# Weight tiles of a hybrid SSD/GLA decoder step: a ring of six half tiles, each with its own transfer, in place of three whole ones

## The chip, the cores and the metric

The kernel runs on one core of one Trainium2 chip. The metric is the device time of one execution in microseconds (us). A core has TensorE (PE, matmuls; its weight loads are the profile's row PEld), VectorE (DVE), ScalarE (ACT) and GpSimd (POOL), and SyncE (SP), which here only issues transfers. Transfers issued by SP and by POOL run on the same 16 DMA engines. PE reads its operands from the on-chip memory (SBUF) and writes accumulators (PSUM).

## The reference

One decoder layer over a prompt of 256 tokens and eight sample sequences of 4 tokens, 288 columns in all, with the same weights: parallel Mamba-2 (SSD) and GLA branches, gated and merged, cross-attention into 256 memory tokens, and a convolutional FFN. Cut to what matters here, the products with weights:

```python
p_mem_k, p_mem_v = _mem_kv(mem_prompt, norm_mem, w_ck, w_cv)
...
xn = _rmsnorm(x, p['norm_mix'])
z, xbc, dt_raw, q, k, v, r, g_lr, gate_a, gate_b = _split(xn @ p['w_in'], IN_SIZES)
...
branch_a = u @ p['w_ssd_out']
...
branch_b = o @ p['w_gla_out']
merged = jax.nn.sigmoid(gate_a) * branch_a + jax.nn.sigmoid(gate_b) * branch_b
h = x + merged @ p['w_mix_out']
h = h + _cross_attend(_rmsnorm(h, p['norm_cross']), mem_k, mem_v, p['w_cq'], p['w_co'])
up = _rmsnorm(h, p['norm_ffn']) @ p['w_up']
up, ffn_conv_new = _causal_dwconv(up, ffn_conv, p['ffn_conv_w'], p['ffn_conv_b'])
a, gt = jnp.split(up, 2, axis=-1)
h = h + (jax.nn.silu(gt) * a) @ p['w_down']
```

Everything is float32. The model width is 2048, the FFN's 5632 (11264 columns of `w_up`).

## The kernel before

Every weight is read from HBM once, as float32, and split into two float32r parts, `whi` (the rounded weight) and `wlo` (what is left); activations are kept split the same way. A product is three matmuls: `whi` with the high part (L147), `whi` with the low part (L148), `wlo` with the high part (L151).

`wload` (L108) gives one raw tile: a buffer of the pool tag `raw`, of which there are RB = 3, and a transfer on SP's queue (L114). `proj_w` (L132) walks over k, the rows of the weight, in tiles of four blocks of 128 rows by 256 columns, 512 KB. It splits each tile in two steps of two blocks: `wsplit` (L100) has ACT cast `whi` (L103) and DVE subtract `wlo` (L105), both 128x512, from five buffers each (WB = 5). For each step PE runs 2 column tiles x 2 blocks x 3 = 12 matmuls of 128 x 288. Two steps share one raw tile, so its buffer is free for the next load when the second step's `wlo` has been computed.

`mem_proj` (L299) computes the memory's keys and values. Its tiles are two blocks of 128 rows by 512 columns, 512 KB too, split block by block; the very first tile is loaded with one transfer for each block (`apart`), since nothing else can start before it. `dt_load` (L482) fills a raw tile of 112 columns for the time steps and the GLA gate with two small transfers (L485) and repeats some columns on POOL (L488).

The order of work on each engine is set by the program's scheduler, which runs a timeline simulation of the instructions; the first `mem_proj` is kept in the order written. Generators of projections are woven with the scans (`weave`, L178), so that PE has matmuls between dependent steps. SP's queue is in order: a load that waits for a buffer holds all that is queued behind it, the state's stores (L915, L1199) among them, and a store that waits for its data holds the loads behind it. POOL's queue carries the loads of states, caches and memory.

Names that the prediction uses: `sin` are rows of the SSD state, updated on DVE (L910) and stored by SP (L915). `xqm` are masked copies of the sample queries in cross-attention (L1508), which ACT and DVE make and the score matmuls (L1529) read; `os` (L1610), `co` and `qh` (L194) are copies and splits in the same place. `sz` (L652) is the activated gate of an SSD group.

Of the kernel before, what the change touches and what calls it, by code (L numbers as in the profile page):

```python
# [16 lines left out]
P = 128  # L17
# [13 lines left out]
FT = FF // P  # L31
BLK = 8
NSQ = 2
RB = 3
WB = 5
STOP = object()
LNEXP = "natural_log_exp_and_others"
# [5 lines left out]
def hybrid_step(ctx: ExitStack, tc: tile.TileContext, I: dict, O: list):  # L43
    ctx.enter_context(tc.block(schedule_with_timeline_sim=True))
    nc = tc.nc
# [15 lines left out]
    def acc_tiles(n):  # L61

        turn[0] += 1
        return [ps.tile([P, 512], F32, tag=f"acc{turn[0] % 2}", bufs=2, name="acc") for _ in range(n)]
# [35 lines left out]
    def wsplit(raw):  # L100

        hi = wp.tile(list(raw.shape), F32R, tag="whi", bufs=WB, name="whi")
        S.copy(hi, raw)  # L103
        lo = wp.tile(list(raw.shape), F32R, tag="wlo", bufs=WB, name="wlo")
        V.tensor_tensor(lo, raw, hi, ALU.subtract)  # L105
        return hi, lo

    def wload(src, apart=False):  # L108
        raw = wp.tile([P, src.shape[1], src.shape[2]], F32, tag="raw", bufs=RB, name="raw")
        if apart:  # L110
            for k in range(src.shape[1]):
                nc.sync.dma_start(out=raw[:, k, :], in_=src[:, k, :])
        else:
            nc.sync.dma_start(out=raw, in_=src)  # L114
        return raw

    late = []
# [9 lines left out]
    def flush():  # L127

        while late:
            late.pop(0)()  # L130

    def proj_w(load, ncol, X, nk, cons, N=T):  # L132

        nt = (ncol + P - 1) // P
        accs = acc_tiles(nt)
        for k0 in range(0, nk, 4):
            kn = min(4, nk - k0)
            raw = load(k0, kn)
            for s0 in range(0, kn, 2):
                hi, lo = wsplit(raw[:, s0:s0 + 2, :])  # L140
                for j in range(nt):
                    m = min(P, ncol - j * P)
                    a = accs[j][0:m, 0:N]
                    cs = slice(j * P, j * P + m)
                    for k in range(2):
                        xh, xl = X(k0 + s0 + k)
                        MM(a, hi[:, k, cs], xh, start=(k0 + s0 + k == 0), stop=False)  # L147
                        MM(a, hi[:, k, cs], xl, start=False, stop=False)  # L148
                    for k in range(2):
                        xh, xl = X(k0 + s0 + k)  # L150
                        MM(a, lo[:, k, cs], xh, start=False, stop=(k0 + s0 + k == nk - 1))  # L151
                    if k0 + s0 + 2 == nk:
                        cons(j, a)
                if k0 + s0 == min(4, nk - 2):
                    flush()
                yield
# [7 lines left out]
    def proj(w, c0, ncol, X, nk, cons, row0=0):  # L164
        def load(k0, kn):
            return wload(rows_of(w, row0, k0, kn, c0, ncol))
        return proj_w(load, ncol, X, nk, cons)
# [104 lines left out]
    with pool("p0") as p0:  # L272
# [9 lines left out]
        def mem_load(k0):  # L282
            cs = slice(k0 * P, (k0 + 2) * P)
            nc.sync.dma_start(out=mt[:, :, cs], in_=I["mem_prompt"][0, :, cs].rearrange("(i p) c -> p i c", p=P))
# [14 lines left out]
        def mem_proj(w, hd, dst, prep=None, hold=None):  # L299

            def feed():
                for k0 in range(0, KT, 2):
                    if prep is not None:
                        mem_load(k0)
                    raw = wload(w[k0 * P:(k0 + 2) * P, 512 * hd:512 * hd + 512].rearrange("(k p) n -> p k n", p=P),
                                prep is not None and k0 == 0)
                    for k in range(2):
                        if prep is not None:
                            prep(k0 + k)
                        yield wsplit(raw[:, k:k + 1, :])  # L310

            accs = acc_tiles(2)
            ws = feed()
            ready = [next(ws) for _ in range(2)] if prep is not None else []
            for kk in range(KT):
                if prep is None:
                    ready.append(next(ws))
                hi, lo = ready.pop(0)
                for m in range(2):
                    ms_ = slice(m * P, (m + 1) * P)  # L320
                    MM(accs[m], mn_hi[:, kk, ms_], hi[:, 0, :], start=(kk == 0), stop=False)  # L321
                    MM(accs[m], mn_lo[:, kk, ms_], hi[:, 0, :], start=False, stop=False)  # L322
                for m in range(2):
                    ms_ = slice(m * P, (m + 1) * P)
                    MM(accs[m], mn_hi[:, kk, ms_], lo[:, 0, :], start=False, stop=(kk == KT - 1))  # L325
                if prep is not None:
                    ready += [w_ for w_ in (next(ws, None) for _ in range(2 if kk == 0 else 1)) if w_]
                yield

            def rows():  # L330
                t = p0.tile([P, 2, 512], F32, tag="mp", bufs=2, name="mp")
                for m in range(2):
                    S.activation(t[:, m, :], accs[m], ACT.Identity, scale=mrs[:, m:m + 1])
                G.dma_start(out=dst[0, :, hd, :].rearrange("(m p) d -> p m d", p=P), in_=t)
            if hold is None:
                rows()
            else:
                hold.append(rows)
# [143 lines left out]
        def dt_load(k0, kn):  # L482
            raw = wp.tile([P, kn, 112], F32, tag="raw", bufs=RB, name="raw")
            for o, c0, n in ((0, O_DT, 32), (32, O_G, 16)):
                nc.sync.dma_start(out=raw[:, :, o:o + n],  # L485
                                  in_=rows_of(I["w_in"], 0, k0, kn, c0, n))
            for k in range(kn):
                G.tensor_copy(raw[:, k, 48:112].rearrange("p (r n) -> p r n", n=16),  # L488
                              raw[:, k, 32:48].unsqueeze(1).to_broadcast([P, 4, 16]))
            return raw  # L490

        def dt_cons(j, a):
# [4 lines left out]
            V.tensor_tensor(lr3[64:80, :], a[64:80], lr3[64:80, :], ALU.subtract)  # L497

        run(proj_w(dt_load, 112, X, KT, dt_cons))

        def dt_prep():
# [908 lines left out]
    for j2 in range(KT // 2):  # L1410
        def cons(j, a, j2=j2):
            added(hx[j2][:, j, :], 2 * j2 + j, a, vec("norm_cross"), hn, acc)
# [238 lines left out]
    for i in range(5):  # L1651
        src = I["ffn_conv_w"][i] if i < 3 else I["ffn_conv_b"] if i == 3 else I["norm_final"]
# [246 lines left out]
```

## Time and profile before

| | us |
|---|---|
| three runs: median (lowest to highest) | 2500.24 (2498.2 to 2500.59) |
| the profiled execution | 2500.31 |
| its span (from the first to the last recorded instruction) | 2498.6 |

How to read it: the span is what the profile's shares refer to; some 1.7 us of the profiled execution lie around it. Busy time of PE is the union of its matmuls, whose ends are modelled. "Idle before" in a row is the time that the engine stood still just ahead of that instruction, and the arrow names what it waited for.

| Stage | from, to (us) | what runs |
|---|---|---|
| memory keys and values | 0 to 186 | `w_ck`, `w_cv`; the input's norm; dt and gate columns at 113 to 122 |
| SSD branch | 186 to 700 | columns of `w_in`, four groups' scans, `w_ssd_out` |
| GLA branch and gates | 700 to 1280 | columns of `w_in`, four heads' scans, `w_gla_out` |
| mix | 1280 to 1380 | `w_mix_out` |
| cross-attention | 1380 to 1646 | `w_cq`, scores and values, `w_co` |
| FFN | 1646 to 2476 | `w_up`, `w_down`, in blocks of eight |
| final norm and stores | 2476 to 2499 | |

The granted clock of PE was 0.997 over the whole span. SP's queue moved 422.35 MB in 408512 packets, POOL's 102.93 MB in 36512.

### The profile page before, as it was taken

The page shows a single profiled execution, that of the slowest core. Times are in us where ns is not written, and L with a number is a line of the kernel's source. Part 1 is how long each engine was busy: PE and PEld are TensorE (multiplying, and loading weights), DVE is VectorE, ACT ScalarE, POOL GpSimd, SP SyncE. Part 2 cuts the span into 40 slices and gives each one's busy share as a digit, 9 for nine tenths or more (in the row PEclk, how much of TensorE's full clock was granted, in tenths as well). Part 3 has the DMA queues.
Part 4 walks back from the last instruction along what each step waited for, and adds up shares of the span by engine and source line. Part 5 has one row for each costly group of instructions (what it writes and reads, how often), then busy time and mean ns, then how long its engine had stood idle before and what let it go on. Part 6 is the DMA issues. An engine that isn't in the chain of part 4 may idle for free.

```text
span 2498.6 us, 50407 instructions
## 1 busy us (share of the span) xinstructions
PE 2480.6 (99%) x18794; PEld 2398.5 (96%) x18794; DVE 1769.2 (71%) x3788; ACT 1332.1 (53%) x2717; POOL 445.3 (18%) x792
## 2 busy tenths in 40 slices
PE   9999999999999999999999999999999999999998
PEld 8889999999999999999999989999999999999998
DVE  6756777797877666777666577667777677675766
ACT  6656647656464655544444545555555454454545
POOL 3102133342311010110111122402111011020012
PEclk9999999999999999999999999999999999999999
DMA  8776587777869686877778599655555555555556
GB/s 246 250 226 203 165 250 203 238 203 221 256 207 290 191 266 188 250 227 237 214 228 271 186 329 334 196 163 173 171 170 171 171 170 172 169 172 170 169 172 171
DMA packets 445302, 528.51 MB, mean 212 GB/s; under 512 B 28492, under 2 KB 391852, under 8 KB 445024
## 3 DMA queue, kind: packets, MB, share of 16 engines
q1 hardware_dynamic: 408512, 422.35, 55.3%
q0 software_dynamic: 36512, 102.93, 12.8%
q8 instruction: 147, 2.41, 0.4%
q14 instruction: 99, 0.81, 0.1%
q10 hardware_dynamic: 32, 0.01, 0.0%
HBM read 476.41 MB, written 48.76 MB: 210 GB/s over the span
## 4 chain that ended last, share of the span: by engine, by line
PE 97%; DMA 1%; DVE 1%; ACT 0%; issue 0%; SPq 0%; DVEq 0%; ACTq 0%
PE acc L148 28%; PE acc L147 27%; PE acc L151 27%; PE acc L321 2%; PE acc L325 2%; PE acc L322 2%; PE mm L1195 1%; PE la L1186 1%; PE la L1529 1%; PE la L1586 1%; DMA raw<-in_w_cq_dram 0%; PE mm L1155 0%; DMA raw<-in_w_in_dram 0%; DMA mt<-in_mem_prompt_dram 0%; PE la L886 0%; PE mm L1169 0%
## 5 line engine op out<-in xcount | busy, mean ns | idle before, releaser
L103 ACT CAST whi<-raw 128x512 fp32r<-128x512 f32 x1464 | 894.0, 617 | 1014.7 <-PE acc L148 728.9
L105 DVE TENSOR_TENSOR wlo<-raw,whi 128x512 fp32r<-128x512 f32 x1464 | 996.2, 688 | 590.7 <-ACT whi L103 577.2
L147 PE MATMUL acc<-xn,whi 128*128 128x288 f32 (+1 forms) x1936 | 540.8, 295 | 3.1 <-DVE sz L652 2.2
L148 PE MATMUL acc<-xn,whi 128*128 128x288 f32 (+1 forms) x1936 | 541.5, 296 | 0.0
L151 PE MATMUL acc<-xn,wlo 128*128 128x288 f32 (+1 forms) x1936 | 409.5, 294 | 0.5 <-DVE wlo L105 0.5
L148 PE MATMUL acc<-hf,whi 128*128 128x288 f32 x1408 | 393.1, 296 | 0.0
L147 PE MATMUL acc<-hf,whi 128*128 128x288 f32 x1408 | 389.0, 292 | 0.0
L147 PEld LDWEIGHTS acc<-xn,whi 128*128 128x128 f32 (+1 forms) x1936 | 363.6, 188 | 8.1 <-ACT whi L103 2.8
L148 PEld LDWEIGHTS acc<-xn,whi 128*128 128x128 f32 (+1 forms) x1936 | 364.1, 188 | 4.4 <-issue 1.5
L151 PEld LDWEIGHTS acc<-xn,wlo 128*128 128x128 f32 (+1 forms) x1936 | 310.4, 188 | 2.2 <-issue 1.1
L151 PE MATMUL acc<-hf,wlo 128*128 128x288 f32 x1408 | 294.6, 290 | 0.0
L148 PEld LDWEIGHTS acc<-hf,whi 128*128 128x128 f32 x1408 | 264.6, 188 | 0.1
L147 PEld LDWEIGHTS acc<-hf,whi 128*128 128x128 f32 x1408 | 264.0, 188 | 0.1
L151 PEld LDWEIGHTS acc<-hf,wlo 128*128 128x128 f32 x1408 | 226.2, 188 | 0.0
L148 PE MATMUL acc<-pr,whi 128*128 128x288 f32 x704 | 196.6, 296 | 0.0
L147 PE MATMUL acc<-pr,whi 128*128 128x288 f32 x704 | 194.7, 293 | 0.0
L1700 POOL COPY fsp<-fst 128x16 f32<-128x16 f32 x88 | 38.8, 444 | 651.9 <-DVE av L1712 430.7
L151 PE MATMUL acc<-pr,wlo 128*128 128x288 f32 x704 | 147.3, 290 | 0.0
L147 PE MATMUL acc<-un,whi 128*128 128x288 f32 x512 | 143.1, 295 | 0.1
L148 PE MATMUL acc<-un,whi 128*128 128x288 f32 x512 | 143.1, 295 | 0.0
L148 PEld LDWEIGHTS acc<-pr,whi 128*128 128x128 f32 x704 | 132.3, 188 | 0.0
L147 PEld LDWEIGHTS acc<-pr,whi 128*128 128x128 f32 x704 | 132.0, 188 | 0.0
(529 smaller groups left out, 4322.8 us busy)
## 6 DMA issues: line engine op xcount, KB each, us to landing
raw<-in_w_in_dram SPq DMA_DIRECT2D x240, 512.0 KB
raw<-in_w_up_dram SPq DMA_DIRECT2D x176, 512.0 KB
raw<-in_w_down_dram SPq DMA_DIRECT2D x88, 512.0 KB
raw<-in_w_cv_dram SPq DMA_DIRECT2D x32, 512.0 KB
raw<-in_w_ssd_out_dram SPq DMA_DIRECT2D x32, 512.0 KB
sin<-in_state_gla_dram POOLq DMA_DIRECT2D x32, 512.0 KB, 6.6
out_dram<-sin SPq DMA_DIRECT2D x32, 512.0 KB
raw<-in_w_gla_out_dram SPq DMA_DIRECT2D x32, 512.0 KB
```

The source lines that it names most:

```text
L103: S.copy(hi, raw)
L105: V.tensor_tensor(lo, raw, hi, ALU.subtract)
L147: MM(a, hi[:, k, cs], xh, start=(k0 + s0 + k == 0), stop=False)
L148: MM(a, hi[:, k, cs], xl, start=False, stop=False)
L151: MM(a, lo[:, k, cs], xh, start=False, stop=(k0 + s0 + k == nk - 1))
L321: MM(accs[m], mn_hi[:, kk, ms_], hi[:, 0, :], start=(kk == 0), stop=False)
L322: MM(accs[m], mn_lo[:, kk, ms_], hi[:, 0, :], start=False, stop=False)
L325: MM(accs[m], mn_hi[:, kk, ms_], lo[:, 0, :], start=False, stop=(kk == KT - 1))
L1186: MM(osa[NS * j:NS * j + NS, :], qdm[:, k, b, :], sins[b][:, k, :], start=False, stop=(q == 1 and k == 0))
L1195: MM(a, kb[:, k * P:(k + 1) * P], vst, start=True, stop=True)
L1529: MM(ssc[NS * c:NS * c + NS, 0:P], xq[:, j, u, :], kt[:, j], start=(j == 0), stop=(j == 15))
L1700: G.tensor_copy(sp[:, :, 0:2], st.rearrange("p (b k) -> p b k", k=2))
```

## The change

A raw tile is halved: two blocks of rows in `proj_w`, one in `mem_proj`, 256 KB each. The ring has six of them, so it takes the same room. Each half is loaded by a transfer of its own and released after one step of the split. `proj_w` asks for both halves of a group of four blocks at once, ahead of the first split; `mem_proj` likewise for its two. `dt_load` is called with two blocks, so it makes twice as many small transfers. The parameter `apart` is gone, since every block of `mem_proj` now has its own transfer. What is computed, and from which bytes, is the same.

```diff
-RB = 3
+RB = 6
...
-    def wload(src, apart=False):
+    def wload(src):
         raw = wp.tile([P, src.shape[1], src.shape[2]], F32, tag="raw", bufs=RB, name="raw")
-        if apart:
-            for k in range(src.shape[1]):
-                nc.sync.dma_start(out=raw[:, k, :], in_=src[:, k, :])
-        else:
-            nc.sync.dma_start(out=raw, in_=src)
+        nc.sync.dma_start(out=raw, in_=src)
         return raw
...
             kn = min(4, nk - k0)
-            raw = load(k0, kn)
+            raws = [load(k0 + s0, 2) for s0 in range(0, kn, 2)]
             for s0 in range(0, kn, 2):
-                hi, lo = wsplit(raw[:, s0:s0 + 2, :])
+                hi, lo = wsplit(raws.pop(0))
...
-                    raw = wload(w[k0 * P:(k0 + 2) * P, 512 * hd:512 * hd + 512].rearrange("(k p) n -> p k n", p=P),
-                                prep is not None and k0 == 0)
+                    raws = [wload(w[k * P:(k + 1) * P, 512 * hd:512 * hd + 512].rearrange("(k p) n -> p k n", p=P))
+                            for k in (k0, k0 + 1)]
                     for k in range(2):
                         if prep is not None:
                             prep(k0 + k)
-                        yield wsplit(raw[:, k:k + 1, :])
+                        yield wsplit(raws.pop(0))
```

Since the scheduler simulates the new transfers, it also places some instructions elsewhere. PE's order is the same but for a few per cent of its rows, in the SSD groups and in cross-attention. Lines after `wload` have numbers lower by four.

The first place is SP's queue around 550 us of the profile before, in the scan of an SSD group: weight loads (`raw_...<-in_w...`) between stores of the updated state (`out_9_dram<-sin`). The numbers behind the names tell one buffer from the next. Before:

```order
L114 DMA raw_7097<-in_w_ssd_out_dram 128x4x256
L114 DMA raw_7141<-in_w_ssd_out_dram 128x4x256
L114 DMA raw_7192<-in_w_in_dram 128x4x256
L915 DMA out_9_dram<-sin_6765 128x2x128 x2
L114 DMA raw_7228<-in_w_in_dram 128x4x256
L915 DMA out_9_dram<-sin_6768 128x2x128 x2
L114 DMA raw_7284<-in_w_in_dram 128x4x256
L114 DMA raw_7330<-in_w_in_dram 128x4x256
```

The same piece of SP's queue with the change:

```order
L110 DMA raw_7486<-in_w_ssd_out_dram 128x2x256
L110 DMA raw_7488<-in_w_ssd_out_dram 128x2x256
L110 DMA raw_7539<-in_w_in_dram 128x2x256
L110 DMA raw_7541<-in_w_in_dram 128x2x256
L110 DMA raw_7577<-in_w_in_dram 128x2x256
L911 DMA out_9_dram<-sin_7096 128x2x128
L110 DMA raw_7579<-in_w_in_dram 128x2x256
L911 DMA out_9_dram<-sin_7096 128x2x128
L110 DMA raw_7635<-in_w_in_dram 128x2x256
L911 DMA out_9_dram<-sin_7099 128x2x128
L110 DMA raw_7637<-in_w_in_dram 128x2x256
L911 DMA out_9_dram<-sin_7099 128x2x128
```

The tile `raw_7228` stood behind two stores; its first half, `raw_7577`, stands ahead of both, its second, `raw_7579`, between them. Loads and stores now alternate one by one.

The second place is ACT in cross-attention, around 1460 us: the casts of weights (`whi`) among the splits of the attention output (`co`) and of the queries (`qh`) and the eight masked copies `xqm`. Before:

```order
L194 CAST co_17475<-mm 128x256
L103 CAST whi<-raw 128x512
L194 CAST co_17475<-mm 128x256
L194 CAST qh<-qs 128x256
L194 CAST co_17475<-mm 128x4x16 x2
L194 CAST qh<-qs 128x256
L1508 COPY xqm_17481<-qsm 32x4x2x4 x8
L103 CAST whi<-raw 128x512 x6
```

With the change:

```order
L190 CAST co_18286<-mm 128x256
L103 CAST whi<-raw 128x512
L190 CAST co_18286<-mm 128x256
L103 CAST whi<-raw 128x512
L190 CAST qh<-qs 128x256
L190 CAST co_18286<-mm 128x4x16 x2
L103 CAST whi<-raw 128x512
L190 CAST qh<-qs 128x256
L1504 COPY xqm_18292<-qsm 32x4x2x4 x8
L103 CAST whi<-raw 128x512 x4
```

Two casts that stood behind the eight copies now stand ahead of them, one of them ahead of the second `qh` directly.

## The prediction

> **What bounds the kernel now.** I read the page first, then the stages, then TensorE's own waits.
>
> ```profile
> span 2498.6 us, 50407 instructions
> ...
> PE 2480.6 (99%) x18794; PEld 2398.5 (96%) x18794; DVE 1769.2 (71%) x3788; ACT 1332.1 (53%) x2717; POOL 445.3 (18%) x792
> ...
> PE 97%; DMA 1%; DVE 1%; ACT 0%; issue 0%; SPq 0%; DVEq 0%; ACTq 0%
> ```
>
> PE is busy 99% of the span, and the chain that ended last runs 97% through it. The number of matmuls doesn't change, so the change can only touch time in which PE is idle: 2498.6 - 2480.6 = 18.0 us. The stages (columns: stretch, its length, then busy time of PE, its weight loads, DVE, ACT and POOL, the granted clock, the share of the DMA engines, GB/s) say where that lies:
>
> ```profile
> 0.00:25.00 25.00, 23.68 (x118) 19.75 (x118) 15.89 (x43) 15.85 (x37) 18.62 (x49) 1.00 0.82 256
> 25.00:186.00 161.00, 160.90 (x739) 132.73 (x738) 105.82 (x197) 96.24 (x193) 10.37 (x23) 1.00 0.78 239
> 550.00:566.00 16.00, 15.06 (x112) 14.67 (x111) 13.84 (x39) 4.78 (x9) 12.69 (x20) 1.00 1.05 300
> 1430.00:1460.00 30.00, 30.00 (x239) 27.18 (x238) 22.40 (x48) 12.29 (x27) 8.29 (x12) 1.00 0.99 365
> 1646.00:2476.00 830.00, 830.00 (x6382) 829.89 (x6381) 591.30 (x1367) 434.34 (x920) 108.71 (x210) 1.00 0.57 172
> 2476.00:2499.00 23.00, 11.48 (x90) 10.96 (x88) 11.53 (x25) 8.67 (x16) 0.00 (x0) 0.77 0.29 105
> ```
>
> 11.5 us of it are the closing stretch (23.00 - 11.48) and 1.3 the opening one; no weight load is late there. 0.1 us is lost from 25 to 186, none in the 830 us of the FFN. What is left is five gaps, seen in PE's timeline (start, length, instruction, in brackets the idle time before it and what ended it):
>
> ```profile
> 563.85 0.40 PE L147 MATMUL acc<-xn,whi 128*128 128x288 f32 x1 [0.94 <-ACT whi L103]
> ...
> 606.42 0.40 PE L147 MATMUL acc<-xn,whi 128*128 128x288 f32 x1 [2.16 <-DVE sz L652]
> ...
> 1257.79 0.40 PE L151 MATMUL acc<-xn,wlo 128*128 128x288 f32 x1 [0.46 <-DVE wlo L105]
> ...
> 1465.72 0.40 PE L147 MATMUL acc<-hn,whi 128*128 128x288 f32 x1 [0.98 <-ACT whi L103]
> ...
> 1576.12 0.67 PE L147 MATMUL acc<-co,whi 128*128 128x288 f32 x3 [0.86 <-ACT co L194]
> ```
>
> Together 0.94 + 2.16 + 0.46 + 0.98 + 0.86 = 5.4 us. That is all a better supply of weights could win.
>
> **The FFN, where nothing moves.** Waits of ACT and of SP's queue in that stage and in the whole run (total us, times, longest):
>
> ```profile
> ACT whi L103 <- PE acc L148: 359.3, 416, 1.7
> ...
> ACT whi L103 <- DMA raw<-in_w_down_dram: 2.2, 1, 2.2
> ...
> SPq L114 <- DVE wlo L105: 1073.6, 431, 13.3
> ...
> SPq L915 <- DVE sin L910: 32.3, 28, 4.7
> ```
>
> There ACT waits 416 times for PE to give a `whi` buffer back and once, 2.2 us, for a weight tile. The five split buffers are full, so neither a sooner nor a slightly later landing reaches PE. 830 us / 528 half tiles = 1.57 us of PE each.
>
> **The change part by part.** Prices of a transfer and of its issue:
>
> ```profile
> L114 SPq DMA_DIRECT2D raw<-in_w_up_dram x176: 367/368/368, 1646.0 to 2367.9; - x176
> ...
> raw<-in_w_in_dram SPq DMA_DIRECT2D x240, 512.0 KB
> ...
> sin<-in_state_gla_dram POOLq DMA_DIRECT2D x32, 512.0 KB, 6.6
> ...
> sqr<-in_state_ssd_dram POOLq DMA_DIRECT2D x128, 64.0 KB, 5.6
> sin<-in_state_ssd_dram POOLq DMA_DIRECT2D x32, 256.0 KB, 5.8
> ```
>
> *Added: transfers.* 1464 casts `whi<-raw` stand for as many halves: 728 weight tiles become 1456, the first of which was already loaded in two; the dt/gate columns' 8 transfers become 16. So 727 + 8 = 735 more. At 368 ns an issue (the half-size one is not in the trace; the duration is the same from minimum to maximum for 512 KB) that is 270 us of SP's queue. Cover: SP already waits 1073.6 us for slots, and in the FFN two issues take 0.74 of each 3.14 us. On the path: 0. Without the cover one more issue would lie before a late half, 0.37 us.
>
> *Moved: landing.* POOL's loads land 5.6, 5.8 and 6.6 us after issue at 64, 256 and 512 KB: a half should land about 0.8 us sooner than a tile. With one tile being split, the old ring has two tiles on the way, 6.6 / 2 = 3.3 us a tile against the 3.14 that PE takes; the new one has four or five halves, 5.8 / 4 = 1.45 us a half against 1.57. The stream has more slack, not less. The Trainium skill (DMA: Bandwidth & Descriptors, Anatomy of one DMA) speaks against small transfers: about 2.0 us fixed plus bytes at 436 GB/s. By it, an estimate, a tile takes 3.2 us and a 256 KB half 2.6; if transfers didn't overlap, halves would then come slower than PE takes them (the last rival). The trace's landings are longer than that fit, and depend as little on size.
>
> *Moved: release.* A slot is free after one `wlo`, not after two. Where it counts, 550 to 566 us (DMA share 1.05):
>
> ```profile
> 550.79 0.70 DVE L105 TENSOR_TENSOR wlo<-raw,whi 128x512 fp32r<-128x512 f32 x1
> ...
> 553.05 0.70 DVE L105 TENSOR_TENSOR wlo<-raw,whi 128x512 fp32r<-128x512 f32 x1
> ...
> 553.77 9.31 DMA raw<-in_w_in_dram
> ...
> 563.18 1.14 ACT L103 CAST whi<-raw 128x512 fp32r<-128x512 f32 x2 [6.04 <-DMA raw<-in_w_in_dram]
> 563.83 0.69 DVE L105 TENSOR_TENSOR wlo<-raw,whi 128x512 fp32r<-128x512 f32 x1 [2.16 <-ACT whi L103]
> ```
>
> The load issued at 553.77 waited for the second `wlo` of its slot's old tile; it landed 9.31 us later, and PE's gap at 563 is its price. As two halves the first can go after the `wlo` that ended at 551.49, 2.3 us sooner, with 256 KB instead of 512 to land. In SP's new order that half stands ahead of the two stores that the tile stood behind, and its second half behind one. It needs to be 0.94 us sooner: gap gone, -0.94 us. Bounds: 0 (the one store is late, 4.7 us at the longest, and holds the second half) and -0.94. DVE, next in line, stood idle for 2.16 us before its `wlo` at 563.83, so it isn't late next.
>
> In cross-attention (1430 to 1460 us, share 0.99) the same holds, and the order of ACT changed:
>
> ```profile
> 1445.53 1.27 DVE L105 TENSOR_TENSOR wlo<-raw,whi 128x512 fp32r<-128x512 f32 x2
> ...
> 1446.23 12.11 DMA raw<-in_w_cq_dram
> ...
> 1458.44 0.62 ACT L103 CAST whi<-raw 128x512 fp32r<-128x512 f32 x1 [6.49 <-DMA raw<-in_w_cq_dram]
> ...
> 1463.21 1.81 ACT L1508 COPY xqm<-qsm 32x32 f32<-32x32 f32 x8
> 1465.05 3.23 ACT L103 CAST whi<-raw 128x512 fp32r<-128x512 f32 x6
> ```
>
> Here a tile landed 12.11 us after issue, then eight `xqm` copies held ACT until 1465.02 with the next cast behind them; PE's 0.98 us gap ends with that cast. In the new order seven casts, not five, stand between the `os` copy and the `xqm` copies, so PE has two more halves in hand: -0.98 us. Bounds: -0.98, and a loss, since the `xqm` copies are now queued behind two more casts that may wait for a transfer (the slower rival). I take the gain: the first half of the late tile no longer waits for the tile's second `wlo`, and the next tile's slot likewise.
>
> From 25 to 186 us (a half is one row of 512 columns there, 256 KB too) earlier halves can close the 0.10 us lost: -0.10. The other three gaps end with an accumulator's consumer or a cast behind other work on DVE and ACT; I leave them. The wider reorder of PE, DVE and ACT touches a few per cent of their rows, in the SSD groups and in cross-attention; new or lost gaps there of the size of the old ones, 0.5 to 2.2 us, either way: 0.
>
> Sum: -0.94 - 0.98 - 0.10 = -2.0 us. The profiled execution took 2500.31 us (1.7 around its span), the median of the runs is 2500.24, so nothing is to be shifted: 2498.3 us.
>
> **The rivals.**
>
> *No gain* (0.24). Halves mostly go out in pairs, and the stretches with late tiles have their DMA engines full (1.05, 0.99): then the bytes decide and not the release, or a new gap takes the old one's place. 2500.3 us.
>
> *All five gaps close* (0.08). For it: earlier supply moves ACT and DVE ahead everywhere. Against: three of the gaps don't end with a transfer. 2500.3 - 5.4 - 0.1 = 2494.8 us.
>
> *ACT stuck behind a half that hasn't landed* (0.14), the slower side. Place: the casts that moved ahead of `qh` and `xqm` in cross-attention. ACT works in order, PE's scores need `xqm`, and the wait for a transfer was 6.49 us there. It decides once a moved cast waits longer than PE's split halves last; two halves are 3.1 us. One such wait uncovered: 2500.3 + 6.5 = 2506.8 us; one for each of three heads: 2519.8. Against: the six casts after the copies ran 3.23 us without a wait, so the data was there.
>
> *Halves land no faster than tiles and only two at a time* (0.02). 5.8 / 2 = 2.9 us a half instead of 1.57 makes loading the bound: 2500.3 + 1464 x 1.33 = 4447 us. Against: the old ring would then have run at 3.3 us a tile in the FFN, and ACT waited once there. The Trainium skill's fit (same page and section) would make it 2.6 us a half and 1464 x 2.6 = 3806 us of loading, an estimate; no run here shows transfers that don't overlap.
>
> **How the numbers follow.** The forecast, both gaps closed, has 0.52. It and "no gain" lie within 0.2% (5 us, about what a measurement of this kernel tells from no change): 0.76. Faster by more: 0.08. Slower by more: 0.14 + 0.02 = 0.16. The range goes from all gaps closed to one uncovered wait on ACT: 2494.5 to 2507 us.
>
> **What would show it.** Right: PE busy still 2480 to 2481 us; no gap at the place of 563.85 and of 1465.72; ACT's 6.04 and 6.49 us waits for transfers shorter than 3; issues of about 368 ns for 256 KB, twice as many; no new wait of ACT for `w_up` or `w_down`. Wrong: PE idle behind `xqm` or a cast that waits for a transfer; casts in the FFN waiting for DMA; PE's busy time itself changed by more than 5 us, which nothing here foresees.

## The result and the profile after

| | before | after |
|---|---|---|
| median of 22 runs each, us | 2499.66 | 2495.32 |
| lowest to highest, us | 2496.06 to 2507.47 | 2491.65 to 2499.58 |
| ratio (95% interval) | | 0.9977 (0.9970 to 0.9984) |
| the profiled execution, its span, us | 2500.31, 2498.6 | 2495.92, 2494.2 |

The medians are 4.3 us apart; the ratio, which sets each run against runs of the kernel before on the same chip, makes it 0.23% or 5.7 us (4.0 to 7.5): small, but its whole interval lies below 1. The forecast was 2498.3 us, a gain of 2.0. The page of the kernel after, its first rows, its chain and its SP queue:

```profile
span 2494.2 us, 52102 instructions
...
PE 2477.1 (99%) x18794; PEld 2396.1 (96%) x18794; DVE 1772.6 (71%) x3788; ACT 1342.0 (54%) x2717; POOL 444.7 (18%) x792
...
q1 hardware_dynamic: 420272, 422.39, 56.4%
...
PE 98%; DMA 1%; DVE 1%; ACT 0%; issue 0%; POOL 0%; DVEq 0%; POOLq 0%; ACTq 0%
```

The span fell by 4.4 us, but PE's idle time only from 18.0 to 17.1 (2494.2 - 2477.1). The other 3.5 us were taken out of busy time (2480.6 to 2477.1) with the same 18794 matmuls. SP's queue carries 11760 more packets, 16 for each of the 735 added transfers, and the same bytes to 0.04 MB. Prices of an issue, from SP's rows by weight (shortest, middle and longest ns; from, to):

```profile
L110 SPq DMA_DIRECT2D raw<-in_w_up_dram x352: 367/368/861, 1640.5 to 2364.0; - x176
...
L110 SPq DMA_DIRECT2D raw<-in_w_ck_dram x64: 327/328/1497, 1.3 to 160.2; - x64
```

An issue of 256 KB takes, in the middle, the 368 ns that one of 512 KB took, 328 in the memory stage; the longest are now longer. The stretches that the prediction quoted, with the same columns:

```profile
25.00:186.00 161.00, 161.00 (x740) 133.32 (x739) 107.66 (x197) 98.50 (x193) 11.86 (x23) 1.00 0.77 239
...
550.00:566.00 16.00, 16.00 (x120) 15.82 (x120) 15.89 (x42) 5.59 (x10) 12.91 (x20) 1.00 1.09 304
...
1430.00:1460.00 30.00, 30.00 (x239) 27.22 (x238) 25.63 (x63) 14.74 (x35) 5.73 (x8) 1.00 1.02 381
...
1646.00:2476.00 830.00, 830.00 (x6383) 829.89 (x6382) 592.20 (x1367) 434.03 (x919) 106.09 (x210) 1.00 0.58 171
```

From 550 to 566 us PE is busy throughout where it stood for 0.94; the FFN holds one matmul more in 830 us, which is nothing. ACT's timeline at the two places of the late tiles shows why (the last brackets are its idle time and what ended it):

```profile
562.74 0.62 ACT L103 CAST whi<-raw 128x512 fp32r<-128x512 f32 x1 [1.28 <-DMA raw<-in_w_in_dram]
...
1451.91 0.62 ACT L103 CAST whi<-raw 128x512 fp32r<-128x512 f32 x1 [1.71 <-DMA raw<-in_w_cq_dram]
...
1457.90 0.62 ACT L103 CAST whi<-raw 128x512 fp32r<-128x512 f32 x1 [0.95 <-DMA raw<-in_w_cq_dram]
1458.85 1.85 ACT L1504 COPY xqm<-qsm 32x32 f32<-32x32 f32 x8
1460.73 2.18 ACT L103 CAST whi<-raw 128x512 fp32r<-128x512 f32 x4
```

The waits of 6.04 and 6.49 us are 1.28 and 1.71, and the `xqm` copies run behind a cast that waited 0.95 and a split of the queries. What is left of PE's old gaps:

```profile
605.72 0.40 PE L143 MATMUL acc<-xn,whi 128*128 128x288 f32 x1 [2.87 <-DVE sz L648]
...
1572.19 0.80 PE L143 MATMUL acc<-co,whi 128*128 128x288 f32 x4 [0.86 <-ACT co L190]
```

No gap stands at 563, 1257 or 1465 us. Three small ones are new, of 0.48, 0.39 and 0.57 us at 445, 1544 and 1561 us; the second trace of this kernel has none of them. The gap behind `sz` grew from 2.16 to 2.87 us, since PE comes to it 1.4 us sooner (602.85 for 604.26) and `sz` only 0.7.

**Where busy time went.** In the mix (1280 to 1380 us) PE does nothing but matmuls of 128 x 288. The stretch from 1300 to 1360 us of it, before and then after:

```profile
1300.00:1360.00 60.00, 60.00 (x458) 60.00 (x457) 39.17 (x71) 30.32 (x58) 9.32 (x15) 1.00 0.78 262
```

```profile
1300.00:1360.00 60.00, 60.00 (x463) 60.00 (x463) 40.05 (x73) 30.89 (x59) 10.61 (x16) 1.00 0.83 264
```

Both are 100% busy at the full granted clock, yet one holds 458 matmuls and the other 463: 131.0 and 129.6 ns each. The starts of the matmuls say it exactly: twelve of them, one split of a weight, take 1580 ns in the one and 1560 in the other, and either rhythm is kept for hundreds of matmuls. In the execution before, the switch to 1580 comes with the gap of 0.46 us at 1257 us and lasts through the mix to 1436; after, that gap is missing and 1560 lasts to 1401. Behind these places both executions have pieces of either rhythm, and 1580 alone from some 1530 us to the FFN. The Trainium skill (Perfetto Trace Analysis, Identifying the Most-Contended Engine) says that busy time of matmuls is a poor measure, because they are pipelined, and that the matmul work done in a stretch and the share of weight loads are the good ones. The trace agrees on the busy time and on the work done, which is the count of matmuls here, 458 and 463; the share of weight loads tells nothing, 60.00 of 60.00 us in both rows.

### The profile page after: what moved, and what is told of

Same layout as the page of the kernel before. It is cut to its first block, busy times and chain, and to the rows that moved or that the text cites. A ratio compares the mean times of both kernels' runs of the same rounds, so it can differ in the third digit from the quotient of the medians.

```text
span 2494.2 us, 52102 instructions
## 1 busy us (share of the span) xinstructions
PE 2477.1 (99%) x18794; PEld 2396.1 (96%) x18794; DVE 1772.6 (71%) x3788; ACT 1342.0 (54%) x2717; POOL 444.7 (18%) x792
## 4 chain that ended last, share of the span: by engine, by line
PE 98%; DMA 1%; DVE 1%; ACT 0%; issue 0%; POOL 0%; DVEq 0%; POOLq 0%; ACTq 0%
PE acc L144 28%; PE acc L143 28%; PE acc L147 27%; PE acc L317 2%; PE acc L321 2%; PE acc L318 2%; PE mm L1191 1%; PE la L1182 1%; PE la L1582 1%; PE la L1525 1%; PE mm L1151 0%; DMA vc<-in_cache_mem_v_dram 0%; DMA raw<-in_w_in_dram 0%; PE la L882 0%; PE mm L1161 0%; PE mm L1165 0%
```

## The experiments

To compare stages I took, in each run's trace, the start of the same matmul by its place in PE's order: the 1000th (end of the memory stage), the 8900th and the 10000th (around the mix), the 12400th (ahead of the FFN) and the last. Each column is the time from the mark before, each row one execution; a pair of transposes that an edit added is not counted:

| kernel | to 1000 | to 8900 | to 10000 | to 12400 | to last |
|---|---|---|---|---|---|
| before | 209.84 | 1038.87 | 145.46 | 261.62 | 832.62 |
| before again | 210.78 | 1041.15 | 145.50 | 261.50 | 832.62 |
| after | 208.37 | 1038.94 | 143.00 | 261.55 | 832.61 |
| after again | 207.91 | 1036.65 | 142.99 | 259.86 | 832.62 |
| tiles in two transfers | 208.47 | 1039.53 | 142.99 | 263.24 | 832.68 |
| the same again | 208.00 | 1038.27 | 142.99 | 262.50 | 832.61 |
| memory stage alone in two | 208.15 | 1037.28 | 142.99 | 263.08 | 832.71 |
| projections alone in two | 209.32 | 1037.04 | 143.01 | 264.84 | 832.62 |
| pair ahead of the mix | 210.30 | 1038.64 | 144.57 | 264.45 | 832.62 |
| pair ahead of `w_co` | 207.84 | 1038.39 | 142.99 | 259.16 | 832.43 |
| stall of twelve | 208.60 | 1039.29 | 142.99 | 261.70 | 835.73 |
| stall of sixteen | 208.33 | 1036.72 | 142.99 | 262.70 | 849.52 |
| half ring of five | 209.87 | 1038.38 | 142.99 | 265.17 | 832.62 |
| half ring of four | 223.24 | 1053.94 | 151.95 | 268.80 | 832.62 |

The profiled pair's 3.94 us are 1.47 in the memory stage and 2.46 in the mix; the FFN gives nothing. Two parts of the table come from the clock and not from the kernels. By the traces' records the full clock is granted from 7.16 and 5.22 us on in the two executions of before, from 6.41 and 5.55 us on in those of after, so its start varies for one and the same kernel. In the profiled pair it comes 0.7 us sooner, and the matmul with number 40 starts at 8.90 us for 9.26; so some 0.4 of the 1.47 is none of the change's doing. And behind the gap at `sz`, near 605 us, the clock falls in some executions of a kernel and not in others. One fall is a granted 0.72 over 6 us, which costs 0.28 x 6 = 1.7 us. The column to 8900 holds one fall in both executions of before, the first of after, the second with tiles in two transfers, the pair ahead of `w_co` and the ring of five, two in the first with tiles in two transfers and in the stall of twelve, and none in the others that have six halves or three tiles.

**How steady is a profile? The kernel before, unchanged.** No edit.

> The kernel before, unchanged, for a second trace. If the gaps belong to the program: the same idle gaps of TensorE near 563, 604, 1257, 1465 and 1575 us, and twelve weight matmuls take 1560 ns up to 1257 us and 1580 ns from there to 1677 us. If they are chance: other gaps or other places. Time 2496 to 2503 us.

One run took 2503.43 us. PE's waits in it (total us, times, longest):

```profile
PE acc L147 <- DVE sz L652: 2.2, 1, 2.2
PE acc L321 <- ACT whi L103: 1.4, 2, 0.7
PE mm L1822 <- DVE h L1788: 1.2, 1, 1.2
...
PE acc L147 <- ACT co L194: 0.9, 1, 0.9
```

Of the five gaps that the prediction added up, only those behind `sz` and `co` are here again. Two behind a late weight are elsewhere, in the memory stage at 50 and 54 us, none stands at 563, 1257 or 1465, and six others are 0.2 to 0.6 us long. PE's timeline at 50 us:

```profile
50.88 0.50 PE L321 MATMUL acc<-whi,mn_hi 128*128 128x512 f32 x1 [0.67 <-ACT whi L103]
...
54.57 0.50 PE L321 MATMUL acc<-whi,mn_hi 128*128 128x512 f32 x1 [0.69 <-ACT whi L103]
```

The mix took 145.50 us again, but not for the rhythm: most of it ran at 1560. It lost its time where a tile of `w_mix_out` came late. ACT waited 35.9 us in 11 waits for that weight (9.4 in 6 the first time). One of these places in the timelines of ACT, of the weight loads and of PE, and then the window:

```profile
1335.60 0.62 ACT L103 CAST whi<-raw 128x512 fp32r<-128x512 f32 x1 [5.61 <-DMA raw<-in_w_mix_out_dram]
...
1339.20 0.30 PEld L151 LDWEIGHTS acc<-mx,wlo 128*128 128x128 f32 x2 [0.33 <-DVE wlo L105]
...
1339.20 0.53 PE L151 MATMUL acc<-mx,wlo 128*128 128x288 f32 x2
...
1300.00:1360.00 60.00, 59.91 (x455) 59.21 (x454) 34.40 (x65) 25.94 (x51) 9.17 (x14) 1.00 0.77 248
```

The weight load waits 0.33 us for `wlo`, and PE's row shows no gap there: a matmul is recorded as 0.29 us long where the next one starts 0.13 us behind it, so a short wait disappears in the overlap. The stretch is 59.91 us busy and holds 455 matmuls. Late weights cost time inside PE's busy row too.

The other executions tell how often a gap comes at the places that the prediction named (us; whole tiles in the projections in the first four rows):

| kernel | near 563 | near 1257 | near 1465 |
|---|---|---|---|
| before | 0.94 | 0.46 | 0.98 |
| before again | none | none | none |
| pair ahead of the mix | 0.45 | 0.59 | 0.56 |
| memory stage alone in two | 0.87 | none | 0.46 |
| tiles in two transfers, the same again, projections alone in two | none | none | 0.46, none, 0.66 |
| ring of six halves (after, again, and with the pair or a stall), five executions | none | none | none |

So the places are real, but whether a tile is late there, and by how much, is a matter of chance, and one trace shows a sample of it.

**Is it the rhythm alone? The kernel before with a pair of transposes ahead of the mix.** `nudge` is the kernel's own helper, which puts two small transposes between matmuls; the FFN has one already.

```diff
+        if j2 == 0:
+            nudge(P)
         run(proj(I["w_mix_out"], 256 * j2, 256, mx, KT, cons))
```

> The kernel before with one more pair of TensorE transposes of the identity, whose result nobody reads, early in the w_mix_out stage (near 1281 us); nothing else moves. If TensorE has two steady rhythms (1560 and 1580 ns for twelve matmuls), a gap can switch it to the slower one and an interposed pair back: 1560 ns from 1281 to about 1400 us, 120 us x 1.27% = 1.5 us less, ratio 0.9994. If the 1580 ns come from something else in that stage (DMA traffic, the tiles): no change of the rhythm, and 0.1 to 0.3 us more.

2502.11 us in the median of 11 runs, ratio 1.0005 (0.9997 to 1.0014). In the trace the gap near 1257 us is here again, 0.59 us, and 1580 begins with it; the pair at 1295.64 us switched it to 1560, and the mix took 144.57 instead of 145.46 us. But cross-attention took 264.45 and the whole was not faster. The rhythm can be switched by what stands between matmuls; as an edit by itself it is worth nothing here.

**Landing without release: whole tiles, each in two transfers.** The ring of three, and the release after the second `wlo`, stay.

```diff
-            nc.sync.dma_start(out=raw, in_=src)
+            n = src.shape[1] // 2
+            for k in (0, n):
+                nc.sync.dma_start(out=raw[:, k:k + n, :], in_=src[:, k:k + n, :])
```

> The kernel before with its three whole tiles, each half loaded by a transfer of its own; only the release stays whole. If sooner landing of the halves is what helps: about 2495.5 us, as with the change, the start 1 us faster, no wait of ACT for the second half. If the release by halves (more bytes on the way) is what helps: the start's share of 0.6 to 1.0 us alone, about 2498.7 us, and the long waits of ACT for transfers near 563 and 1458 us stay. If only the other order of the instructions helps: anything, with gaps at new places.

2496.93 us, 0.9989 (0.9980 to 0.9998), 11 runs. The edit also makes the scheduler place some instructions elsewhere. ACT's waits for the largest weight:

```profile
ACT whi L103 <- DMA raw<-in_w_in_dram: 52.0, 41, 3.7
```

They were 78.6 us in the kernel before, and in the kernel after:

```profile
ACT whi L103 <- DMA raw<-in_w_in_dram: 44.1, 27, 3.6
```

Taken over again, with the same edit:

> All whole tiles loaded by halves once more, for a narrower interval beside the others of this call. Landing alone carries half of the gain: ratio 0.9985 to 0.9992 again. Landing alone carries all of it and the first 11 runs were unlucky: 0.9975 to 0.998.

2497.11 us, 0.9987 (0.9978 to 0.9996), 11 runs. The 22 runs of this kernel have a mean of 2497.2 us, 94 runs of the kernel before, over all comparisons, one of 2500.6: sooner landing, in the order that the scheduler then chose, gives about 3.4 us. ACT's waits for all weights together go the same way: 157 to 191 us in the four traces with whole tiles in the projections, 107 and 90 with all tiles in two transfers, 58 to 65 in three traces with six halves (after, again, the pair ahead of `w_co`).

**Supply worse: a half ring of four.** Two thirds of the room.

```diff
-RB = 6
+RB = 4
```

> The change with four half tiles in the ring in place of six: the release stays fine, the bytes on the way fall from five halves to three. If the bytes on the way carry the gain: slower than the kernel before, 2505 us or more, ACT waiting for transfers where the DMA engines are full (20 to 60, 110 to 186, 550 to 566, 1430 to 1550 us). If the fine release alone is enough: 2495 to 2498 us.

2538.21 us, 1.0153 (1.0139 to 1.0167), 4 runs. The page:

```profile
span 2540.2 us, 52086 instructions
...
PE 2498.5 (98%) x18794; PEld 2400.5 (94%) x18794; DVE 1768.7 (70%) x3788; ACT 1332.2 (52%) x2717; POOL 438.9 (17%) x792
```

Ahead of the FFN PE stands still for 31.2 us, where in the profiled execution before it is 6.9. The span is 41.6 us longer, and 17.9 of these (2498.5 - 2480.6) are busy time. Its windows show both at once, from 25 to 110 us (before, that stretch held 380 matmuls in 84.90 us):

```profile
25.00:110.00 85.00, 80.57 (x349) 65.02 (x348) 49.65 (x80) 47.23 (x96) 2.23 (x3) 0.98 0.75 231
```

349 matmuls in 80.57 busy us are 231 ns each, before 223: what runs between gaps runs slower, part of it at a lower clock (0.98), and short waits can hide in it as in the mix above. In cross-attention the slower rival's mechanism shows: at 1545 us PE waits 2.10 us for `xqm`, which stood on ACT behind a cast that waited 2.60 us for `w_cq`. The FFN took the same 832.62 us with four halves as with six.

**Between: a half ring of five.**

```diff
-RB = 6
+RB = 5
```

> The change with five half tiles in the ring, one less. With four it was 38 us slower than the kernel before, with six 5.5 us faster. If the bytes on the way set a threshold: between them, 2497 to 2508 us, with gaps only where the DMA engines are full (memory stage, 550 to 566 us, cross-attention). If six was already more than enough: 2494 to 2496 us.

2498.43 us, 0.9992 (0.9983 to 1.0001), 11 runs: not told from three whole tiles, with 1280 KB instead of 1536. The gain of the six needs the sixth. This kernel has the landing and the release by halves, and PE's order differs from that of the kernel after in 124 of 18794 places, so neither the finer steps nor the order give the gain without the room.

**The kernel after, again.** No edit.

> The changed kernel, unchanged, for a second trace and more times. If the ring's finer steps make the supply steady: 2494 to 2497 us again, ratio 0.997 to 0.9985, again no gap of TensorE before 440 us and none at 1257 us, the position after the memory stage 1 us or more ahead of the kernel before. If the first trace was luck: gaps in the memory stage as in the traces of before.

2493.44 us, 0.9976 (0.9967 to 0.9986), 10 runs: the result repeats. With the runs above, 32 runs of the kernel after have a mean of 2494.9 us, 2.2 below the 22 with whole tiles in two transfers (standard error 0.5, from a spread of 1.9 and 1.8). That is left for the sooner release and for what the scheduler placed differently in the two kernels, which were not told apart.

**The rhythm in the kernel after: a pair ahead of `w_co`.** There twelve matmuls take 1580 ns from 1574 us to the FFN.

```diff
+    nudge(P)
     run(*wo[:5])
```

> The change with one more pair of TensorE transposes, read by nobody, ahead of the third product of w_co (near 1580 us), where twelve matmuls take 1580 ns until 1675 us; nothing else moves. If an interposed pair switches TensorE to the 1560 ns rhythm: 95 us x 1.27% = 1.2 us less than the change, 2494.1 us; if it stays at 1580: 0.2 us more.

2493.62 us, 0.9973 (0.9964 to 0.9982), 11 runs. The trace shows the switch to 1560 at the pair, at 1580 us. From the gap behind `co` to the FFN it takes 79.13 us, the two traces of the kernel after 79.66 and 79.67, so the pair brings 0.5 us; in the time this can't be told from the kernel after beside it (0.9976).

**The price of a rhythm: one stall in the FFN.** In the kernel after, one cast of the FFN is repeated, so that PE runs out of `whi` once. Twelve repeats, and sixteen; they compute the same again.

```diff
-        S.copy(hi, raw)
+        splits[0] += 1
+        for _ in range(13 if splits[0] == 1000 else 1):
+            S.copy(hi, raw)
```

> The change with one stall in the FFN, near 1750 us: one of the 1464 casts of ACT is done thirteen times over (twelve more, 12 x 0.62 = 7.4 us), some 5 us of which the split buffers cover, so TensorE should stand still once for 2 to 3 us. If a stall costs its own length alone: 2497.5 to 2499 us, twelve matmuls 1560 ns before and behind it. If a stall can switch TensorE to the slower rhythm, which then stays through the FFN: up to 1.27% of the 720 us behind it more, 9 us, 2507 us.

> As the stall of twelve, with sixteen more casts (9.9 us): a gap of some 5 us. Length alone: 2500 us. With the slower rhythm behind it: up to 2509 us.

Twelve: 2507.39 us in the median of 10 runs, 1.0018 (1.0006 to 1.0030), in two groups with nothing between: three runs from 2499.13 to 2500.18, seven from 2506.28 to 2508.83. Sixteen, one run: 2511.98. PE's stall in the one (an execution of the lower group), then in the other:

```profile
1758.98 0.40 PE L147 MATMUL acc<-hf,whi 128*128 128x288 f32 x1 [2.80 <-ACT whi L107]
```

```profile
1759.74 0.61 PE L147 MATMUL acc<-hf,whi 128*128 128x288 f32 x1 [5.40 <-ACT whi L107]
```

The windows behind it, twelve:

```profile
1755.00:1775.00 20.00, 17.20 (x133) 16.97 (x132) 16.04 (x43) 13.84 (x33) 4.71 (x2) 1.00 0.55 170
...
1800.00:2400.00 600.00, 600.00 (x4617) 600.00 (x4617) 428.29 (x999) 306.40 (x651) 71.39 (x144) 1.00 0.57 171
```

and sixteen:

```profile
1755.00:1775.00 20.00, 15.26 (x100) 15.26 (x101) 13.41 (x32) 12.17 (x26) 1.10 (x2) 0.83 0.50 151
...
1800.00:2400.00 600.00, 600.00 (x4560) 600.00 (x4559) 424.12 (x996) 303.68 (x650) 68.74 (x140) 1.00 0.56 168
```

After the stall of 5.40 us the rhythm is 1580 to the end: 4560 matmuls in 600 us, not 4617. Over the 717 us from 1759 to 2476 that is 717 x 20 / 1580 = 9.1 us. Its FFN is 16.9 us longer than that of the kernel after (849.52 against 832.61): 5.4 are the stall, 9.1 the rhythm and 2.2 a lower clock right behind the stall (0.83; 100 matmuls took 15.26 us instead of 13.0). The profiled execution with twelve repeats kept 1560 and lost 3.1 us in its FFN. The two groups of its runs are some 8 us apart, which fits a switch in seven runs of ten; a trace of one of the seven was not taken.

**Which stage's halves count?** Whole tiles again, loaded in two transfers only in the memory stage, then only in the projections.

```diff
-                                prep is not None and k0 == 0)
+                                True)
```

> The kernel before, with the two rows of every memory tile (w_ck, w_cv) loaded by two transfers; ring, release and the order on TensorE stay. If sooner landing is what helps in the memory stage: no gap of TensorE before 186 us and a position 1.0 to 2.5 us ahead of the kernel before there, nothing changed behind it: 2498 to 2499 us, ratio 0.9990 to 0.9996. If it takes the release by halves: as the kernel before, ratio 1.000.

```diff
+        elif src.shape[1] == 4:
+            for k in (0, 2):
+                nc.sync.dma_start(out=raw[:, k:k + 2, :], in_=src[:, k:k + 2, :])
```

> The kernel before, with the 512 KB tiles of the projections loaded by two transfers each and the memory tiles as they were. Sooner landing in the projections: no gap at 563 and 1257 us, as with all tiles split, and the memory stage as before: 2498 to 2500 us, ratio 0.9992 to 1.0. Together with the memory tiles alone the two should make what all tiles split made (0.9989).

Memory stage alone: 2498.41 us, 0.9993 (0.9984 to 1.0002). Projections alone: 2499.65 us, 0.9995 (0.9987 to 1.0004). 11 runs each. Neither is told from no change by itself; together (-0.0007 - 0.0005) they make the -0.0011 and -0.0013 of both. The traces are clearer on the first: the four executions with whole tiles in the memory stage (before twice, the pair, projections alone) reach the 1000th matmul at 209.3 to 210.8 us, mean 210.1; the eight with halves there and the full room, those with an edit in a later stage among them, at 207.8 to 208.6, mean 208.2. Of these 1.9 us the start of the full clock makes some 0.4 (on the mean at 6.7 us in the four, 5.9 in the eight), so the stage is worth about 1.5 us. The edit that splits its transfers alone leaves PE's order as it was, ACT's in all but six places and DVE's in all but two, so there it is the landing.

A ring of four whole tiles or of eight halves has no room in SBUF. A release by halves with whole landing was not tried, nor was the new order with the old tiles.

## Why the prediction was right in kind and wrong in size

**Right in kind.** The gaps at 563.85 and at 1465.72 us are gone, in all five traces with six halves; the first is gone with sooner landing alone, so the release was not needed there, while the second comes in two of three traces with landing alone; ACT's 6.04 and 6.49 us waits are below 3; twice as many issues cost their 368 ns each and nothing that PE's path shows; the FFN is the same to 0.01 us; the slower rival did not come, though the ring of four shows that it was a real one. Halves are not too slow: the rival that let only two of them fly at a time is refuted by the FFN and by every stage.

**Wrong in size, 2.0 us for 4.3 between the medians and 5.7 by the ratio.** A gain that a measurement tells from no change was given a chance of 0.08. Three steps failed.

- "The number of matmuls doesn't change, so the change can only touch time in which PE is idle." It does not follow. Of 4.4 us of the span, 3.5 came out of busy time. The same matmuls run at 1560 or 1580 ns for twelve, and at a lower clock behind some gaps; a short wait for a weight hides in the overlap of the matmuls; so late supply costs more than the gaps it leaves: with the half ring of four, 17.9 of 41.6 us are busy time. The prediction itself named a change of PE's busy time as what "nothing here foresees". (Of its 18.0 us, the 11.5 of the closing stretch reach 0.4 us past the end of the span; the forecast does not use them.)
- "-0.10" for 25 to 186 us, and "no weight load is late there" for the first 25. The term was mis-sized: the memory stage gave about 1.5 us. The trace of before shows little idle time there; the next one shows two gaps of 0.7 us, and from 25 to 110 us it holds 371 matmuls where the first held 380 and both traces of the kernel after 382. In the first 25 us no weight is late, but in both traces of before a load of PE waits 0.6 and 0.7 us for a tile of the memory (`mt`), which comes on POOL's queue; in those of after none does.
- "Together 0.94 + 2.16 + 0.46 + 0.98 + 0.86 = 5.4 us. That is all a better supply of weights could win." These were one execution's gaps. Only 2.16 and 0.86, which don't hang on a transfer, came in every execution of before's order. At 563 and at 1465 us a gap came in three of the four executions with whole tiles, of 0.45 to 0.98 us, and none in the second trace of before, which lost its time in other places. So the sum of -0.94 and -0.98 was not the price of two places but a sample of a price spread over the program. And the 0.46 at 1257, which the prediction left, was gone too, with the slower rhythm that came with it: 2.46 us in the mix alone. Both traces with a gap there run at 1580 behind it, and none of the ten others with the full room does; in the second trace of before, late tiles cost the mix as much.

**The split between the two terms.** Landing in halves gives about 3.4 us, release and new order together about 2.2 more; they add up to 5.6, beside 5.7 by the ratio. The table of stages says where, as means over few executions. To the 8900th matmul, with 1.7 us taken off for each fall of the clock, the four with whole tiles in the projections take 1037.2 to 1039.5 us and the eight with halves and the full room 1035.9 to 1037.2, 1.5 us less on the mean. The mix takes 142.99 to 145.50 with whole tiles and 143.0 with halves, 1.6 less on the mean. In cross-attention sooner landing gives nothing: 263.5 us on the mean of three, with whole tiles 262.7; the ring of six takes 261.5 on the mean of the four executions without a pair there. So the 2.2 us are to be looked for in cross-attention, and with the memory stage the four add up to 1.5 + 1.5 + 1.6 + 1.2 = 5.8 us. The Trainium skill (DMA: Bandwidth & Descriptors, Bandwidth) advises transfers of 1 MiB or more for the sake of the rate. Here the DMA engines are full only in short stretches (1.09 from 550 to 566 us, 0.58 in the FFN), and the measurement goes the other way: transfers of 256 KB beat those of 512 KB in the same ring (0.9989, 0.9987), and the ring of halves in the same room does more (0.9977). What the room is worth is seen with the ring in halves: four, five and six slots give 1.0153, 0.9992 and 0.9977.

## What to carry to other kernels

Where a ring of prefetched tiles feeds a busy TensorE, make the unit of transfer and of release as small as the consumer's step: the same room then holds more steps in flight, here for one 368 ns issue on a queue that had time. Take several traces before pricing late transfers by their gaps, since a place can have a gap in three of four. And don't take a full busy row as a floor: count the matmuls in equal stretches, since the same ones can run at two speeds, and wait, under 100%.

## What the hardware showed that was not expected

- Twelve float32r matmuls of 128 x 288 take 1560 or 1580 ns (130.0 or 131.7 each), both at a granted clock of 1.00 and fully busy. A rhythm lasts until something comes between: a stall of 5.40 us switched it to the slower for the rest of the FFN, 9.1 us; two small transposes switched it back, ahead of the mix and ahead of `w_co`. What decides whether a stall switches it stays open: one of 2.80 us did not, in its trace, while seven of ten runs of that kernel look as if it did.
- A stall can lower the granted clock behind it, but its length alone doesn't say so. After 2.80 us in the FFN it was 1.00, after 5.40 it was 0.83 over 20 us. Behind the stand at `sz`, near 605 us, it was 0.72 over six us in the kernel before (2.16 us) and in the kernel after (2.87 us), and 1.00 in the kernel after again, with the same 2.87 us. The row of before, three of after, and the row of after again:

```profile
606.00:612.00 6.00, 5.58 (x32) 5.58 (x33) 1.59 (x7) 2.26 (x5) 0.00 (x0) 0.72 0.12 43
...
600.00:606.00 6.00, 3.13 (x25) 2.90 (x24) 4.92 (x11) 4.92 (x13) 0.00 (x0) 1.00 0.70 230
606.00:612.00 6.00, 6.00 (x37) 6.00 (x37) 1.26 (x5) 2.33 (x4) 0.00 (x0) 0.72 0.02 6
612.00:620.00 8.00, 8.00 (x63) 8.00 (x62) 7.91 (x18) 6.88 (x14) 0.00 (x0) 1.00 0.14 39
...
606.00:612.00 6.00, 6.00 (x51) 6.00 (x49) 3.04 (x8) 3.91 (x8) 0.00 (x0) 1.00 0.00 0
```

In the kernel after 37 matmuls take 6.00 us there and 63 the 8.00 behind, though not all of one form: at the later pace 37 take 4.7 us, so that gap cost about 1.3 us beside its own 2.87 (1.7 by the clock alone). The fall comes in both kernels and is no part of what the change does. The Trainium skill (TensorE: Matmul & The Clock Gate, The HAM clock gate) has the clock halved after an idle window of about 3.4 us that runs freely. The 5.40 us fit that, and so does the chance at 605 us from one execution to the next; the 2.16 us there show that a shorter stand can be enough.
